# A hybrid HGRN2 / SSD block on one core: operands of the output projection turned as queued small products, and three smaller moves

## The chip, the cores and the metric

The kernel runs on one core of one Trainium2 chip, as one program. A core has a matrix engine (TensorE, PE in the profile, with PEld for its weight loads), VectorE (DVE), ScalarE (ACT), GpSimd (POOL) and SyncE (SP); each takes its own instructions strictly in their order and waits on semaphores for the others. Data move between HBM and the on-chip memory by DMA transfers, which SP, ACT or POOL issue. The metric is the time of one execution on the device, in microseconds (us); lower is better.

## The reference

One layer of a streaming encoder, for one sequence of 512 tokens of width 2048, all in float32:

```python
mod = silu(c) @ w_mod + b_mod                 # 2048 -> 6 x 2048
shift1, scale1, gate1, shift2, scale2, gate2 = split(mod, 6)
h = rms_norm(x, norm1_w) * (1 + scale1) + shift1
q, f, i, g, z, xbc, dt = split(h @ w_in)      # 4 x 1024, 1024, 2048, 16 columns
o_a = hgrn2_mixer(q, f, i, g)                 # 8 heads of 128, chunks of 64
o_b = ssd_mixer(z, xbc, dt)                   # 16 heads of 64 in 4 groups, state 128
x = x + gate1 * (concat(o_a, o_b) @ w_out)
h = rms_norm(x, norm2_w) * (1 + scale2) + shift2
u = causal_dwconv(h @ ffn_w_up)               # 2 x 5632, width 3
x = x + gate2 * ((silu(u_gate) * u_val) @ ffn_w_down)
return rms_norm(x, final_norm_w)
```

The SSD heads need, for each head and chunk, a matrix of decays `exp(acum[t] - acum[s])`, where `acum` is the running sum over time of `dt * a` of that head. The HGRN2 heads are a gated linear recurrence with its own decay for each of 128 channels; the kernel builds their attention matrix by doubling levels (1, 2, 4, ... 64).

## The kernel before

**Layout.** Tokens are 4 tiles of 128 (`NT`), the width 16 tiles of 128 (`KT`). For float32 accuracy every large product is three: an operand is split into a rounded part `hi` and a rest `lo`, and `mm3` issues hi x hi, hi x lo and lo x hi into the same PSUM bank (L168 to L170). Weights come through `wchunk`: SP loads two row tiles by 512 columns into a `raw` buffer (5 of them, L148), ACT rounds it to `whi` (L163), VectorE takes the difference `wlo` (L164); two `hi` and two `lo` buffers. `feat_group` and `tok_group` run a group of 512 columns over all 16 row tiles, eight chunks of 24 large products each, into 4 of 6 PSUM banks (`ACC`). Two more banks (`MIS`) serve all small products.

**Order of the work.** First the input is normed and transposed and the modulation of the first norm is summed; the SSD columns and the first half of the values `v` follow (`SEGMENTS`), then `v_group(1)`, four groups for the HGRN gates and queries (two heads each), two groups of `z`, two groups of `g`, the output projection (4 groups), the second norm, and the gated ConvFFN, which takes the second half of the time and which the change does not touch.

**The queue of small products.** The head mixers (`ssd_mix`, `hgrn_mix`) are Python generators that yield after small pieces. They stand in `waiting`; `small()`, called after every three large products, advances one of at most two active generators by one piece, so that small products stand between large ones in the program. A piece may ask to be left alone for some calls (`yield 3`). `drain()` advances until nothing is left.

**Modulation in the background.** `mod_unit` sums 512 columns of one of the six modulation vectors: eight loads `m` of 512 KB on SP (L184), which share the `raw` buffers, 16 multiply-adds on VectorE (L189, L191), then eight products with a column of ones that turn the sums (L203), and the addition into `modT` (L206). It yields after each load; the last multiply-adds and the column products follow in one step. `tick()`, called for each weight chunk, gives out `rate` steps: 0.5 in the gate and query groups, 1.5 from `z` to the output projection. `tick(99)` after the output projection does what is left. Twelve units run this way (scale2, gate1, shift2); four more (gate2) run in the FFN.

**The parts that the change touches.** `ssd_dt` turns the running sums so that they stand in 64 rows of 128 (chunk and head), and writes them to a DRAM tile `acrow` (L401). `decay(h)` in `ssd_mix` reads for one head four rows of 512 bytes, repeated for all 128 partitions, into a buffer `mm` (L436, issued by POOL), and makes the decay matrix from it (L439 to L443); L489 and L499 multiply with it and with the state, L494, L501 and L505 add the results into `y`. At the end of `hgrn_mix` three key tiles are transposed (L585), copied by ACT (L587) and multiplied into the states (L592), which VectorE evacuates (L595, L597); then ACT copies the reversed halves of the attention and query tiles into forward order (`fwd`, L602), and L612 and L615 form the output. `make_mix(kt)` transposes one of the 16 operand tiles of the output projection from `y` or `o` (four transposes, L859) and splits it (ACT L860, VectorE L861). In the kernel before it is a plain function, called in bursts of four behind the first `g` group, and of four and eight behind the second, where the queue is drained first. The residual `x` is loaded again behind that (`x1`, 4 x 1 MB on SP) and turned by `turn_x` through the queue (L897); `turn_x1` turns the result back (L905).

**What sets the final order.** A scheduler orders each engine's instructions before the run: it reckons with modelled durations and takes, of those that are ready, the one that stands first in the program (`tc.high_priority` moves some ahead). On the chip that order is fixed. Buffers come from pools by tag: 13 large ones `e`, 2 `y`, 2 `a`, and 9 of 512 columns (`T`); a new tile waits until an earlier one is released.

Of the kernel before, what the change touches and what calls it, by code (L numbers as in the profile page):

```python
# [7 lines left out]
F32 = mybir.dt.float32  # L8
F32R = mybir.dt.float32r
# [25 lines left out]
def hybrid_block_kernel(  # L35
# [140 lines left out]
    def mod_unit(part, j4):  # L176
# [4 lines left out]
        for q in range(9):  # L181
            if q < 8:
                m = wst.tile([P, 2, 512], F32, tag="raw", name=nm("m"))
                nc.sync.dma_start(out=m, in_=wmod[q * 256:(q + 1) * 256, c0:c0 + 512].rearrange(  # L184
                    "(k p) n -> p k n", p=P))
            for k in range(2 if q else 0):
                kt = 2 * q - 2 + k
                if kt == 0:
                    V.tensor_scalar(out=acc, in0=last[:, k, :], scalar1=cT[:, kt:kt + 1], scalar2=None, op0=ALU.mult)  # L189
                else:  # L190
                    V.scalar_tensor_tensor(out=acc, in0=last[:, k, :], scalar=cT[:, kt:kt + 1], in1=acc,  # L191
                                           op0=ALU.mult, op1=ALU.add)
            last = m
            if q < 8:
                yield
        ps = MIS()
# [160 lines left out]
    drm = ctx.enter_context(tc.tile_pool(name="drm", bufs=1, space=bass.MemoryType.DRAM))  # L357
    acrow = drm.tile([64, P], F32, tag="acrow", name="acrow")
    dtt = CT([P, 64], "dtt")
# [4 lines left out]
    def ssd_dt(src):  # L364
# [35 lines left out]
        V.tensor_copy(out=ar[0:64, 0:P], in_=pr[0:64, 0:P])  # L400
        nc.gpsimd.dma_start(out=acrow, in_=ar[0:64, 0:P])  # L401

    def ssd_mix(g):
# [29 lines left out]
        def decay(h):  # L433
            hh = 4 * g + h
            m = mt[h] = T("mm")
            nc.gpsimd.dma_start(out=m.rearrange("p (c t) -> p c t", c=4),  # L436
                                in_=acrow.rearrange("(c h) t -> h c t", h=16)[hh].partition_broadcast(P))
            m8 = m.rearrange("p (a t) -> p a t", a=8)
# [112 lines left out]
    def hgrn_mix(h, f, k, q):  # L551
# [12 lines left out]
        for lv in LEVELS:  # L564
# [15 lines left out]
            V.tensor_tensor(out=fb[:, :, :, 0, 0], in0=fb[:, :, :, 0, 0], in1=fb[:, :, :, 1, 0], op=ALU.mult)  # L580
            yield 3
        kt_ = T("Kt")[:, 0:3 * P]
        ps = MIS()
# [12 lines left out]
        for cch in (1, 2):  # L596
            V.scalar_tensor_tensor(out=st[:, cch * P:(cch + 1) * P], in0=st[:, (cch - 1) * P:cch * P],  # L597
                                   scalar=f[:, slot(cch).start:slot(cch).start + 1], in1=ps[:, cch * P:(cch + 1) * P],
                                   op0=ALU.mult, op1=ALU.add)
        fwd = T("fwd")  # L600
        for n, o in enumerate((att, q)):
            A.copy(out=fwd[:, n * 256:(n + 1) * 256].rearrange("p (c s) -> p c s", c=2),  # L602
                   in_=o[:, 256:512].rearrange("p (c s) -> p c s", c=2)[:, :, ::-1])

        def tokens(o, n, cch):
            return fwd[:, n * 256 + cch // 2 * P:n * 256 + (cch // 2 + 1) * P] if cch % 2 else o[:, slot(cch)]

        yield 1
# [52 lines left out]
    def feat_group(pieces, blocks, chunk_src=win, kts=range(0, KT, 2), accs=None, span=(0, KT),  # L661
                   rhs=None, kk_in=False):

        accs = accs or [ACC() for _ in blocks]
        rh, rl = rhs or (hhi, hlo)
        for k0 in kts:
            hi, lo = wchunk(chunk_src, k0, 2, pieces)
            tick()
# [181 lines left out]
    def make_mix(kt):  # L850
        q, j = divmod(kt, 4)
        if q not in mt_:
            mt_[q] = (E(F32R, "mhi"), E(F32R, "mlo"))
        hi, lo = mt_[q][0][:, j * 512:(j + 1) * 512], mt_[q][1][:, j * 512:(j + 1) * 512]
        mhi[kt], mlo[kt] = hi, lo
        src, col, w = (ov, kt, gnT[:, kt:kt + 1]) if kt < 8 else (yv, kt - 8, snT[:, kt - 8:kt - 7])
        ps = MIS()
        for t in range(NT):
            PE.transpose(out=ps[:, t * P:(t + 1) * P], in_=src(t)[:, col * P:(col + 1) * P], identity=ident)  # L859
        A.activation(out=hi, in_=ps, func=AF.Copy, scale=w)  # L860
        V.scalar_tensor_tensor(out=lo, in0=ps, scalar=w, in1=hi.bitcast(F32), op0=ALU.mult, op1=ALU.subtract)  # L861

    for j in range(2):
        accs = tok_group(win, C_G + 512 * j, hhi, hlo, list(range(KT)))
        if j:
            drain()
        for kt in range(8 + 4 * j, 12 + 4 * j):
            make_mix(kt)
        for t in range(NT):
# [7 lines left out]
    order = list(range(8, 16)) + list(range(0, 8))  # L877
    for kt in range(8):
        make_mix(kt)
    x1 = []  # L880
    for t in range(NT):
        x1t = E(name="x1")
        nc.sync.dma_start(out=x1t, in_=xd[t * P:(t + 1) * P, :])
        x1.append(x1t)
    x1T = []
    for q in range(4):
        x1T.append(E(name="x1T", tag=("y", "y", "a", "e")[q]))
    ssq2 = E(name="ssq2", tag="a")[:, 0:512]

# [3 lines left out]
    def turn_x(kt):  # L893

        ps = MIS()
        for t in range(NT):
            PE.transpose(out=ps[:, t * P:(t + 1) * P], in_=x1[t][:, kt * P:(kt + 1) * P], identity=ident)  # L897
            yield 0
        A.copy(out=x1f(kt), in_=ps)

    def turn_x1(q, t, bank):
# [8 lines left out]
    for n in range(4):  # L910
        accs = feat_group([(512 * n, 512)], [bl(i) for i in range(4)], chunk_src=wout, kts=order[::2], span=(8, 8),
                          rhs=(mhi, mlo), kk_in=True)
        with tc.high_priority(offset=2000 if n == 3 else 0):
# [168 lines left out]
```

## Time and profile before

| | us |
|---|---|
| median of 3 runs | 2491.99 (2491.88 to 2496.45) |
| the profiled execution | 2497.32 |
| its span, first to last instruction | 2495.6 |
| TensorE busy | 2416.4 (97%) |
| VectorE busy | 1490.2 (60%) |
| ScalarE busy | 783.7 (31%) |
| GpSimd busy | 55.7 (2%) |
| mean granted clock of TensorE | 0.991 |

In the rows of the profile `L436` is line 436 of the kernel, `mm<-acrow` means that the instruction writes tile `mm` and reads `acrow`, and `x16` that there were 16 of them. A large product shows as some 0.39 us busy but the next one starts 0.23 us after it, since products overlap; a busy TensorE is therefore not yet one at its peak. A row of the waits says which engine and tile waited, for whom, and how long in all, how often, and the longest. The granted clock is the share of TensorE's full clock in a stretch. A chain of waits follows the work that ended last back to what released it.

### The profile page before, as it was taken

What the parts mean: (1) busy time and instruction counts of PE and PEld (TensorE: products, weight loads), DVE (VectorE), ACT (ScalarE), POOL (GpSimd) and SP (SyncE); (2) the same over time, 40 slices, a digit from 0 to 9 for tenths busy, and PEclk for the clock granted to TensorE, in tenths of its full rate; (3) what the DMA queues carried; (4) which work ended last, traced back from release to release, by engine and by line L of the source; (5) the groups of instructions that cost most, each with busy time, mean ns of one, the idle gap of its engine ahead of it and who ended that gap; (6) DMA issues with size and microseconds to landing.
All of it is one profiled execution on the core that took longest, in us unless ns stands there. A gap on an engine that the chain in (4) does not pass through costs nothing.

```text
span 2495.6 us, 28998 instructions
## 1 busy us (share of the span) xinstructions
PE 2416.4 (97%) x11071; PEld 1987.7 (80%) x11071; DVE 1490.2 (60%) x2262; ACT 783.7 (31%) x1135; POOL 55.7 (2%) x80
## 2 busy tenths in 40 slices
PE   6999998999999999999999999999999999999998
PEld 5777877788777777887888888888888888888887
DVE  6884866666776656668536363636354545454557
ACT  6323422333332322433232222222222222222323
POOL 4000000000000000000000000000000000000000
PEclk9999999999999999999999999999999999999999
DMA  9883575344555656366333323233333333332332
GB/s 289 257 273 105 116 128 107 90 118 135 168 161 187 243 189 199 121 220 219 93 101 93 101 93 100 94 98 96 96 99 95 100 94 101 93 101 93 102 127 85
DMA packets 262823, 335.86 MB, mean 135 GB/s; under 512 B 18092, under 2 KB 182524, under 8 KB 261404
## 3 DMA queue, kind: packets, MB, share of 16 engines
q1 hardware_dynamic: 260432, 327.42, 41.8%
q0 software_dynamic: 1568, 4.31, 2.3%
q10 hardware_dynamic: 684, 2.28, 0.3%
q8 instruction: 87, 1.43, 0.2%
q14 instruction: 52, 0.43, 0.1%
HBM read 329.72 MB, written 4.23 MB: 134 GB/s over the span
## 4 chain that ended last, share of the span: by engine, by line
PE 76%; DMA 11%; DVE 9%; issue 2%; ACT 2%; POOL 0%; SPq 0%; DVEq 0%; ACTq 0%; POOLq 0%
PE acc L170 24%; PE acc L168 24%; PE acc L169 24%; DMA m<-in_w_mod_dram 8%; DVE wlo L164 3%; DVE macc L191 2%; DMA raw<-in_w_in_dram 1%; DVE macc L240 1%; DMA x<-in_x_dram 1%; ACT whi L163 1%; PE mis L570 1%; POOL rstd L267 0%; DMA mm<-acrow 0%; PE mis L612 0%; DVE att L577 0%
## 5 line engine op out<-in xcount | busy, mean ns | idle before, releaser
L164 DVE TENSOR_TENSOR wlo<-raw,whi 128x1024 fp32r<-128x1024 f32 (+1 forms) x408 | 490.3, 1203 | 707.7 <-ACT whi L163 703.2
L163 ACT CAST whi<-raw 128x1024 fp32r<-128x1024 f32 (+2 forms) x416 | 424.6, 1022 | 1304.4 <-PE acc L169 512.2
L168 PE MATMUL acc<-hhi,whi 128*128 128x512 f32 x1920 | 770.1, 402 | 10.7 <-ACT whi L163 6.1
L170 PE MATMUL acc<-hhi,wlo 128*128 128x512 f32 x1920 | 750.1, 393 | 3.1 <-DVE wlo L164 3.1
L169 PE MATMUL acc<-hlo,whi 128*128 128x512 f32 x1920 | 751.7, 392 | 0.0
L168 PEld LDWEIGHTS acc<-hhi,whi 128*128 128x128 f32 x1920 | 362.2, 189 | 88.2 <-ACT whi L163 10.2
L170 PEld LDWEIGHTS acc<-hhi,wlo 128*128 128x128 f32 x1920 | 362.3, 189 | 83.0 <-DVE wlo L164 6.1
L169 PEld LDWEIGHTS acc<-hlo,whi 128*128 128x128 f32 x1920 | 362.8, 189 | 69.5 <-issue 1.2
L191 DVE SCALAR_TENSOR_TENSOR macc<-m,cT,macc 128x512 f32<-128x512 f32 x240 | 180.0, 750 | 127.9 <-DMA m<-in_w_mod_dram 124.5
L168 PE MATMUL acc<-whi,act 128*128 128x512 f32 x640 | 249.0, 389 | 0.0
L169 PE MATMUL acc<-wlo,act 128*128 128x512 f32 x640 | 249.0, 389 | 0.0
L170 PE MATMUL acc<-whi,act 128*128 128x512 f32 x640 | 249.0, 389 | 0.0
L168 PE MATMUL acc<-whi,hhi 128*128 128x512 f32 x384 | 163.2, 425 | 0.0
L170 PE MATMUL acc<-whi,hlo 128*128 128x512 f32 x384 | 153.7, 401 | 0.0
L169 PE MATMUL acc<-wlo,hhi 128*128 128x512 f32 x384 | 152.8, 398 | 0.0
L170 PEld LDWEIGHTS acc<-whi,act 128*128 128x128 f32 x640 | 120.1, 188 | 25.0
L168 PEld LDWEIGHTS acc<-whi,act 128*128 128x128 f32 x640 | 120.1, 188 | 24.9
L169 PEld LDWEIGHTS acc<-wlo,act 128*128 128x128 f32 x640 | 120.1, 188 | 24.9
L994 DVE TENSOR_TENSOR g<-acc,gate 128x512 f32<-128x512 f32 x160 | 105.4, 685 | 3.8
L995 DVE TENSOR_TENSOR x<-x,g 128x512 f32<-128x512 f32 x160 | 105.3, 684 | 0.0
L168 PE MATMUL acc<-mhi,whi 128*128 128x512 f32 x256 | 105.2, 411 | 0.0
L170 PE MATMUL acc<-mhi,wlo 128*128 128x512 f32 x256 | 101.1, 395 | 2.3 <-DVE wlo L164 2.3
(274 smaller groups left out, 2193.9 us busy)
## 6 DMA issues: line engine op xcount, KB each, us to landing
raw<-in_ffn_w_up_dram SPq DMA_DIRECT2D x352, 256.0 KB, 2.9
m<-in_w_mod_dram SPq DMA_DIRECT2D x128, 512.0 KB, 4.1
raw<-in_ffn_w_down_dram SPq DMA_DIRECT2D x88, 512.0 KB, 3.6
m<-in_w_mod_dram SPq DMA_DIRECT2D x128, 256.0 KB, 4.2
raw<-in_w_in_dram SPq DMA_DIRECT2D x96, 256.0 KB, 3.9
raw<-in_w_in_dram SPq DMA_DIRECT2D x48, 512.0 KB, 4.0
raw<-in_w_out_dram SPq DMA_DIRECT2D x32, 512.0 KB, 4.5
x<-in_x_dram SPq DMA_DIRECT2D x8, 1024.0 KB, 10.8
```

The lines of the kernel that those rows point to most:

```text
L163: A.copy(out=h_, in_=r_)
L164: V.tensor_tensor(out=l_, in0=r_, in1=h_.bitcast(F32), op=ALU.subtract)
L168: PE.matmul(out=ps, lhsT=lh, rhs=rh, start=first, stop=False)
L169: PE.matmul(out=ps, lhsT=lh, rhs=rl, start=False, stop=False)
L170: PE.matmul(out=ps, lhsT=ll, rhs=rh, start=False, stop=last)
L191: V.scalar_tensor_tensor(out=acc, in0=last[:, k, :], scalar=cT[:, kt:kt + 1], in1=acc, op0=ALU.mult, op1=ALU.add)
L240: V.scalar_tensor_tensor(out=acc, in0=m[:, k, :], scalar=cT[:, kt:kt + 1], in1=acc, op0=ALU.mult, op1=ALU.add)
L570: PE.matmul(out=o, lhsT=kk[:, pr * P:(pr + 1) * P], rhs=halves(q, lv, True, base=pr * P, pairs=1), start=True, stop=True)
L994: V.tensor_tensor(out=m, in0=accs[t], in1=gates[5][:, cs], op=ALU.mult)
L995: V.tensor_tensor(out=x1[t][:, cs], in0=x1[t][:, cs], in1=m, op=ALU.add)
```

## The change

Four edits.

1. **Operands as queued small products.** `make_mix` becomes a generator that yields after each transpose. The eight SSD tiles are queued behind the first `g` group, after a `drain()` that stood behind the second; the eight HGRN tiles are queued behind the second. `need_mix(kt)` advances the queue until a pair of tiles is made; `feat_group` gets a hook `before` that calls it ahead of each chunk of the output projection. The turning of `x` is queued behind the operands, and a loop makes sure that the tiles of `x` that a group adds to have been turned. Some tiles change pools: the last pair of operand tiles is taken from `a`, `x1T` from `y` and `e`, and `ssq2` from `e`.
2. **Head operands ahead.** In `hgrn_mix` the two `fwd` copies stand ahead of the key transposes.
3. **Modulation sums a step later.** `mod_unit` also yields after the last multiply-adds, so that its column products come one step later.
4. **Decay rows by head.** `acrow` is 16 rows of 512 (one for each head); `decay` reads one row of 2 KB for each partition, and ACT issues the load.

```diff
@@ mod_unit
             last = m
-            if q < 8:
-                yield
+            yield
         ps = MIS()
@@
-    acrow = drm.tile([64, P], F32, tag="acrow", name="acrow")
+    acrow = drm.tile([16, S], F32, tag="acrow", name="acrow")
@@ ssd_dt
-        nc.gpsimd.dma_start(out=acrow, in_=ar[0:64, 0:P])
+        nc.gpsimd.dma_start(out=acrow.rearrange("h (c t) -> c h t", c=4), in_=ar[0:64, 0:P])
@@ ssd_mix, decay
-            nc.gpsimd.dma_start(out=m.rearrange("p (c t) -> p c t", c=4),
-                                in_=acrow.rearrange("(c h) t -> h c t", h=16)[hh].partition_broadcast(P))
+            nc.scalar.dma_start(out=m, in_=acrow[hh].partition_broadcast(P))
@@ hgrn_mix
+        fwd = T("fwd")
+        for n, o in enumerate((att, q)):
+            A.copy(out=fwd[:, n * 256:(n + 1) * 256].rearrange("p (c s) -> p c s", c=2),
+                   in_=o[:, 256:512].rearrange("p (c s) -> p c s", c=2)[:, :, ::-1])
...
         kt_ = T("Kt")[:, 0:3 * P]
...
-        fwd = T("fwd")
-        for n, o in enumerate((att, q)):
-            A.copy(out=fwd[:, n * 256:(n + 1) * 256].rearrange("p (c s) -> p c s", c=2),
-                   in_=o[:, 256:512].rearrange("p (c s) -> p c s", c=2)[:, :, ::-1])
...
@@ feat_group
-                   rhs=None, kk_in=False):
+                   rhs=None, kk_in=False, before=None):
...
         for k0 in kts:
+            if before:
+                before(k0)
             hi, lo = wchunk(chunk_src, k0, 2, pieces)
@@ make_mix
-            mt_[q] = (E(F32R, "mhi"), E(F32R, "mlo"))
+            mt_[q] = (E(F32R, "mhi", "a" if q == 3 else "e"), E(F32R, "mlo", "a" if q == 3 else "e"))
...
             PE.transpose(out=ps[:, t * P:(t + 1) * P], in_=src(t)[:, col * P:(col + 1) * P], identity=ident)
+            yield 0
...
+        made.add(kt)
+
+    made = set()
+
+    def need_mix(kt):
+        while not {kt, kt + 1} <= made:
+            small()
 
     for j in range(2):
         accs = tok_group(win, C_G + 512 * j, hhi, hlo, list(range(KT)))
-        if j:
+        if j == 0:
             drain()
-        for kt in range(8 + 4 * j, 12 + 4 * j):
-            make_mix(kt)
+            waiting.extend(make_mix(kt) for kt in range(8, 16))
...
-    for kt in range(8):
-        make_mix(kt)
-    x1 = []
+    waiting.extend(make_mix(kt) for kt in range(8))
+    for kt in range(8, KT, 2):
+        need_mix(kt)
+    x1, x1T, turned = [], [], set()
...
-    x1T = []
-    for q in range(4):
-        x1T.append(E(name="x1T", tag=("y", "y", "a", "e")[q]))
-    ssq2 = E(name="ssq2", tag="a")[:, 0:512]
+
+    sq2 = []
@@ turn_x
+        if kt % 4 == 0:
+            x1T.append(E(name="x1T", tag="y" if kt < 8 else "e"))
...
+        turned.add(kt)
@@ output projection
         accs = feat_group([(512 * n, 512)], [bl(i) for i in range(4)], chunk_src=wout, kts=order[::2], span=(8, 8),
-                          rhs=(mhi, mlo), kk_in=True)
+                          rhs=(mhi, mlo), kk_in=True, before=need_mix)
+        while not set(range(4 * n + 4)) <= turned:
+            small()
+        if not sq2:
+            sq2.append(E(name="ssq2")[:, 0:512])
+        ssq2 = sq2[0]
```

More of the change, by code (lines that the diff above doesn't have):

```diff
@@ L581, in hgrn_mix, with tokens @@
             yield 3
+        fwd = T("fwd")
+        for n, o in enumerate((att, q)):
+            A.copy(out=fwd[:, n * 256:(n + 1) * 256].rearrange("p (c s) -> p c s", c=2),
+                   in_=o[:, 256:512].rearrange("p (c s) -> p c s", c=2)[:, :, ::-1])
+        def tokens(o, n, cch):
+            return fwd[:, n * 256 + cch // 2 * P:n * 256 + (cch // 2 + 1) * P] if cch % 2 else o[:, slot(cch)]
         kt_ = T("Kt")[:, 0:3 * P]
@@ L599, in hgrn_mix @@
                                    op0=ALU.mult, op1=ALU.add)
-        fwd = T("fwd")
-        for n, o in enumerate((att, q)):
-            A.copy(out=fwd[:, n * 256:(n + 1) * 256].rearrange("p (c s) -> p c s", c=2),
-                   in_=o[:, 256:512].rearrange("p (c s) -> p c s", c=2)[:, :, ::-1])
-        def tokens(o, n, cch):
-            return fwd[:, n * 256 + cch // 2 * P:n * 256 + (cch // 2 + 1) * P] if cch % 2 else o[:, slot(cch)]
         yield 1
```

## Prediction

> **What bounds the kernel now.** I read the page's first and fourth parts, then stretches of the span, then TensorE's waits, then the chain inside the worst stretch. The profiled execution took 2497.3 us (its span and 1.7 us around it); the three timed runs have a median of 2491.99, 5.3 us less. My terms come from the trace and are subtracted from the median.
>
> ```profile
> span 2495.6 us, 28998 instructions
> ...
> PE 76%; DMA 11%; DVE 9%; issue 2%; ACT 2%; POOL 0%; SPq 0%; DVEq 0%; ACTq 0%; POOLq 0%
> ```
>
> TensorE carries three quarters of the chain, so only its idle time and its slow clock can be won; the change removes no product. Where that idle time lies, by stretches (columns: us, PE busy, PEld, DVE, ACT, POOL, granted clock, DMA share, GB/s):
>
> ```profile
> 300.00:350.00 50.00, 46.34 (x228) 38.01 (x227) 41.94 (x76) 15.31 (x21) 3.74 (x5) 0.99 0.73 111
> 350.00:400.00 50.00, 47.98 (x239) 38.77 (x239) 34.72 (x61) 13.74 (x19) 2.98 (x4) 0.98 0.55 125
> 400.00:450.00 50.00, 41.31 (x193) 33.72 (x193) 27.80 (x61) 12.71 (x16) 2.99 (x4) 0.94 0.59 105
> 500.00:550.00 50.00, 49.92 (x261) 41.63 (x260) 29.05 (x58) 19.56 (x53) 2.05 (x2) 1.00 0.39 111
> 750.00:800.00 50.00, 47.57 (x222) 39.37 (x221) 30.80 (x52) 14.52 (x24) 2.43 (x2) 1.00 0.59 188
> 800.00:850.00 50.00, 46.96 (x235) 38.47 (x234) 32.67 (x54) 17.46 (x23) 0.00 (x0) 1.00 0.66 224
> 1000.00:1050.00 50.00, 47.28 (x236) 39.82 (x235) 28.33 (x40) 20.73 (x32) 1.01 (x1) 0.97 0.39 122
> ```
>
> 300 to 450, where the SSD heads run between other products, loses 3.7 + 2.0 + 8.7 = 14.4 us of TensorE and, by the granted clock, 50 x (0.01 + 0.02 + 0.06) = 4.5 us more. The turning of the projection operands (750 to 850) loses 2.4 + 3.0. TensorE's own waits name the causes (total, times, longest, us):
>
> ```profile
> PE mis L499 <- DVE y L494: 7.9, 2, 4.2
> PE mis L499 <- DVE yo L501: 4.2, 1, 4.2
> PE mis L612 <- DVE st L597: 3.9, 2, 2.0
> PE mis L859 <- DVE mlo L861: 3.1, 2, 2.4
> PE mis L897 <- DMA x<-in_x_dram: 2.3, 1, 2.3
> PE mis L451 <- DVE cbm L429: 2.0, 2, 1.8
> PE mis L203 <- DVE st L597: 1.4, 1, 1.4
> ```
>
> L499 waits for VectorE to empty one of the two small PSUM banks. Why VectorE is late, the chain from 410 to 450 us says:
>
> ```profile
> 416.65 9.10 DMA m<-in_w_mod_dram
> 425.77 0.75 DVE macc L191
> ...
> 436.99 8.15 DMA mm<-acrow
> 445.16 0.69 DVE mm L439
> ...
> 446.77 0.70 PE mis L499 x2
> ```
>
> VectorE takes its work in order and stands before a modulation load (9.1 us) or a decay row (8.2 us), with the emptying of the bank behind it.
>
> **Decay rows by head.** Each of 16 loads today reads four 512-byte runs for every partition, issued from POOL; after the change it reads one 2 KB run, issued from ACT. The rows it goes by:
>
> ```profile
> q1 hardware_dynamic: 260432, 327.42, 41.8%
> q0 software_dynamic: 1568, 4.31, 2.3%
> q10 hardware_dynamic: 684, 2.28, 0.3%
> ...
> raw<-in_ffn_w_up_dram SPq DMA_DIRECT2D x352, 256.0 KB, 2.9
> m<-in_w_mod_dram SPq DMA_DIRECT2D x128, 512.0 KB, 4.1
> ...
> mm<-acrow POOLq DMA_DIRECT2D x16, 256.0 KB, 9.2
> ```
>
> The same 256 KB land in 2.9 us from SP and in 9.2 from POOL. Per MB, POOL's queue (q0) holds the DMA engines 2.3/4.31 = 0.53% of the span, SP's (q1) 0.13%, ACT's (q10) 0.13%. The 4.2 MB of decay rows thus cost about 2.2% of 2495.6 = 56 us of all engines, within the 160 us from 287 on; at q10's rate 14. So 42 us of engine time come free exactly where the modulation loads land late: a median of 4.1 us, but 9.1 in the chain above. I estimate 4 us to landing (between 2.9 and 9.2, nearer the first, since the queue kind and run length become those of the first). Five us come off each decay wait, and the modulation wait before 425.77 falls to its median. The three L499 waits and L451 sum to 14.1 us with a longest of 4.2: all are shorter than the five us. Bounds: 0 (VectorE's order still sets the waits) to 14.1. I take **10**, because the emptying of a bank still stands behind the decay arithmetic (L439, 0.69 us, and what follows). The slow clock follows the gaps: 0 to 4.5 us, I take **3**.
>
> What the issue costs on ACT, and POOL's issue for comparison:
>
> ```profile
> L259 ACTq DMA_DIRECT2D gate<-in_b_mod_dram x1: 396/396/396, 1039.3 to 1039.3; - x1
> ...
> L436 POOL DMA_DIRECT2D mm<-acrow x16: 747/747/804, 286.7 to 437.0; - x16
> ...
> ACT whi L163 <- PE acc L169: 512.2, 142, 7.4
> ...
> POOL mm L436 <- PE mis L489: 94.3, 5, 54.1
> ```
>
> 0.4 us x 16 = 6.3 us of ACT, which is busy at most 31% here. Behind an issue that waits for its buffer stand the weight casts (L163), for which TensorE waits. On POOL five issues waited for TensorE (L489), harmlessly. ACT's casts themselves wait for TensorE to free the weight buffers (512 us in all), so a hold until an earlier TensorE product costs 0; without that cover, five holds of up to one weight chunk (5.4 us) would cost 27. I take 0. The row write to DRAM (32 KB, now strided) has 24 us until the first read and costs nothing.
>
> **Projection operands as queued small products.** The 16 turnings keep their 64 transposes, 16 ACT copies (L860) and 16 VectorE ones (L861), but go between the big products, one per three. Today they come in bursts of eight and stop when both banks are full:
>
> ```profile
> 774.66 1.04 PE L859 MATMUL mis<-ident,y 128*128 128x128 f32 x8
> ...
> 777.36 0.39 PE L170 MATMUL acc<-whi,hlo 128*128 128x512 f32 x1
> 777.59 0.39 PE L168 MATMUL acc<-whi,hhi 128*128 128x512 f32 x1
> 780.40 0.66 PE L859 MATMUL mis<-ident,y 128*128 128x128 f32 x4 [2.43 <-DVE mlo L861]
> ...
> L615 PE MATMUL mis<-st,fwd x32: 270/274/358, 516.3 to 747.0; 128*128 128x128 f32 x32
> ```
>
> Gone: 3.1 us of L859. The x reload (four of 1 MB on SP) is first used about 40 small products later than today, some 30 us, so 2.3 us of L897 go too. The draining before the operands moves one group forward; the last head product today starts at 747.0 (L615), the first gate group, behind which the draining moves, ends where the first burst starts, at 774.7, so it finds the queue empty: 0. In exchange, two turnings at a time hold both banks, and each of the eight hand-overs needs VectorE on time, in a stretch where it waits for modulation loads. Bounds 0 to 8 x 2.43 = 19.4; nearest are the x turnings (L897), which hand over the same way and wait for their load alone, but ACT empties them. I take 3. Net **-2.4**. The moves between buffer pools keep 13 large buffers in use at most; 0.
>
> **Modulation sums a step later.** No TensorE wait is for a sum of theirs: the only L203 wait is for a bank (1.4 us), and that stays. Each of the 12 units needs 10 steps instead of 9, 120 against 108. Steps given out: 32 chunks at 0.5 and 64 at 1.5, 112. So 8 steps remain after the last chunk and come at once: six 512 KB loads, 14 multiply-adds, 8 column sums. Chunks are 24 products at 0.23 us, 5.4 us; the rows agree, since the last sums stand three chunks ahead of the last output-projection product:
>
> ```profile
> L203 PE MATMUL mis<-ones,macc x96: 164/250/271, 494.7 to 1011.0; 128*128 128x1 f32 x96
> ...
> L191 DVE SCALAR_TENSOR_TENSOR macc<-m,cT,macc x240: 741/752/758, 331.0 to 1169.8; 128x512 f32<-128x512 f32 x120
> ...
> 1027.33 0.40 PE L170 MATMUL acc<-mhi,wlo 128*128 128x512 f32 x1
> ```
>
> 14 x 0.752 = 10.5 us of VectorE around 1010 to 1040. Cover: 21.7 us of VectorE idle in 1000 to 1050, and a DMA share of 0.39. Without it they stand ahead of the second norm, whose statistics and operands are VectorE's: 0 to 10.5, I take **+1**.
>
> **Head operands copied ahead.** Two ACT copies per head (L602, 0.41 us each) go before the key copy. They are off the path: TensorE's waits at L612 are for the state evacuation on VectorE. Bounds: -3.9 (if those waits went) to +0.8 x 8 = 6.4 (if each key copy came that late unhidden; ACT is 39% busy in 500 to 550). I take 0.
>
> ```profile
> L602 ACT COPY fwd<-att x8: 402/406/408, 509.8 to 731.2; 128x256 f32<-128x256 f32 x8
> ```
>
> **Sum:** -10 - 3 - 2.4 + 1 = -14.4; 2491.99 - 14.4 = **2477.6**.
>
> **The rivals.**
>
> *The rows land no sooner.* The same 16 engines serve the same bytes, 55 to 73% busy there; only the issue gets cheaper, 0.35 us at each of four waits, 1.4 us. The time is then 2491.99 - 1.4 - 2.4 + 1 = 2489. For it: modulation loads on the fast queue also took 9 us. Against: q0's fourfold time per MB. The Trainium skill says so in "DMA: Bandwidth & Descriptors", section "Issuing engines are not separate DMA queues": starting a transfer from another engine saves only the issue. Here the run length changes as well, and the row of 9.2 against 2.9 us speaks against it. Chance 0.15.
>
> *All of it goes.* 14.1 + 4.5 + 5.4 us, with no hand-over wait and no tail: 2468. For it: all three causes are late DMAs. Chance 0.2.
>
> *The hand-overs cost more than the rows gain (slower).* Place: the second gate group and the first output group. Each hand-over waits for L861 behind a multiply-add that waits for a load. At 2.43 us plus a full 4.1 us load each, 8 x 6.5 = 52 us, less the 5.4 and 13 that go: +34. With half of them late, 26 - 18.4 = +8, 2500, which I take. It is slower from 18.4/8 = 2.3 us per hand-over on. Against: the scheduled order places a transpose where its bank is reckoned free. Chance 0.1.
>
> **How the numbers follow.** My forecast has 0.55 (2470 to 2487), the others 0.15, 0.2 and 0.1. A measurement here tells 0.2%, 5 us, from no change: same is 2487 to 2497. Faster: 0.55 x 0.95 + 0.2 + a little of the first rival, 0.74. Same: the rest of that rival and of the forecast, 0.15. Slower: 0.11, the last rival and some order that the scheduler upsets. The range 2464 to 2496 takes all four terms at their best, 24 us plus 3.9 of L612, and most of the first rival; it leaves out the slower one.
>
> **What would show it.** Decay rows landing in 3 to 5 us on ACT's queue, L499 waits below 4 us in all, and the granted clock at 0.98 or more in 400 to 450. L859 waits below 3 us and none at L897 for x. A last L203 start within a few us of the last output-projection product, and 1000 to 1050 no worse than 47.3 us of TensorE. I am wrong if L499 waits as before, or if TensorE's waits at L859 and L203 pass 15 us.

## The result

The changed kernel takes 2481.53 us in the median (2478.29 to 2483.98, 5 runs), the kernel before 2496.45 us beside it (2491.88 to 2498.66, 5 runs): a ratio of 0.9947, 95% interval [0.9935, 0.9958]. The prediction was 2477.6 us, 0.9942 of the median it was made against. The profiled execution took 2480.27 us, 1.7 us more than its span.

From the page of the changed kernel, the span, ACT's queue (packets, MB, share of 16 engines) and the chain by engine:

```profile
span 2478.6 us, 28956 instructions
...
q10 hardware_dynamic: 2988, 6.47, 0.8%
...
PE 80%; DMA 8%; DVE 8%; ACT 2%; issue 1%; SPq 0%; POOL 0%; ACTq 0%; DVEq 0%; POOLq 0%
```

From its view of transfers, the decay rows (KB each, median us to landing):

```profile
mm<-acrow ACTq DMA_DIRECT2D x16, 256.0 KB, 4.5
```

They land in half the time, TensorE's share of the chain rises from 76 to 80%, and transfers fall from 11 to 8%. TensorE's own waits for small products, once 7.9 and 4.2 us at L499 (now L497), 3.1 at L859 and 2.3 at L897 (now L905), are these, as far as they bear on the change:

```profile
PE mis L449 <- DVE y L456: 2.9, 2, 1.5
PE mis L914 <- ACT x L916: 2.8, 2, 2.2
...
PE mis L610 <- DVE st L603: 1.5, 2, 1.1
PE acc L914 <- ACT x L916: 1.4, 1, 1.4
PE mis L202 <- DVE mlo L862: 1.3, 1, 1.3
...
PE mis L202 <- ACT o L618: 1.3, 1, 1.3
PE acc L914 <- DVE x1T L930: 0.7, 1, 0.7
...
PE mis L497 <- DVE y L492: 0.5, 1, 0.5
...
PE mis L497 <- DVE yo L499: 0.5, 1, 0.5
```

Where the time went, by stretches: the SSD heads (280 to 460) and the output projection (860 to 1020). The columns are those of the prediction's table. Before:

```profile
280.00:460.00 180.00, 165.63 (x800) 135.32 (x799) 129.28 (x234) 58.49 (x83) 12.02 (x16) 0.97 0.62 116
860.00:1020.00 160.00, 156.28 (x729) 126.72 (x729) 89.95 (x117) 41.87 (x52) 0.00 (x0) 1.00 0.59 191
```

After, with the two stretches that the prediction had named:

```profile
280.00:460.00 180.00, 176.09 (x879) 144.96 (x878) 136.73 (x247) 63.71 (x91) 0.00 (x0) 1.00 0.40 120
860.00:1020.00 160.00, 152.71 (x721) 122.72 (x719) 95.73 (x125) 46.04 (x61) 0.00 (x0) 0.98 0.61 194
...
400.00:450.00 50.00, 49.54 (x249) 40.96 (x248) 31.30 (x68) 18.66 (x29) 0.00 (x0) 1.00 0.39 117
...
1000.00:1050.00 50.00, 45.37 (x235) 37.50 (x235) 43.43 (x64) 25.92 (x39) 1.01 (x1) 1.00 0.49 154
```

In 280 to 460 TensorE's idle time falls from 14.4 to 3.9 us, its clock rises from 0.97 to 1.00, and the DMA engines' share falls from 0.62 to 0.40 at the same bytes per second. Fixed places in the work show how much of that arrives. The groups by line of the kernel before give the first product of the HGRN heads, which follow the SSD heads, and the last one of the output projection (min/median/max ns, first and last start):

```profile
L557 PE MATMUL mis<-q,FK x64: 270/273/324, 460.1 to 681.7; 128*128 128x128 f32 x64
...
L170 PE MATMUL acc<-mhi,wlo x256: 387/389/504, 825.9 to 1027.3; 128*128 128x512 f32 x128
```

The same two places and the last modulation sums in the changed kernel:

```profile
L555 PE MATMUL mis<-q,FK x64: 270/273/321, 445.1 to 668.8; 128*128 128x128 f32 x64
...
L170 PE MATMUL acc<-mhi,wlo x256: 388/393/628, 807.8 to 1011.3; 128*128 128x512 f32 x128
...
L202 PE MATMUL mis<-ones,macc x96: 164/250/352, 494.5 to 1012.2; 128*128 128x1 f32 x96
```

The changed kernel leads by 460.1 - 445.1 = 15.0 us when the SSD heads are done, by 1027.3 - 1011.3 = 16.0 at the end of the output projection, and by 2495.6 - 2478.6 = 17.0 at the end. Nearly all of the gain is made before 445 us. In between, the passage to the second norm gives back 1.6 us: with the large products (L168 to L170) counted in their order, the 3600th, behind that passage, starts 14.4 us earlier than before. The last 17.0 - 14.4 = 2.6 us come in the FFN's first group (below).

### The profile page after: what moved, and what is told of

Its sections match the earlier page's. It is cut to its first block, busy times and chain, and to the rows that moved or that the text cites. A ratio compares the mean times of both kernels' runs of the same rounds, so it can differ in the third digit from the quotient of the medians.

```text
span 2478.6 us, 28956 instructions
## 1 busy us (share of the span) xinstructions
PE 2414.0 (97%) x11071; PEld 1982.7 (80%) x11071; DVE 1494.3 (60%) x2262; ACT 786.4 (32%) x1135; POOL 43.4 (2%) x64
## 3 DMA queue, kind: packets, MB, share of 16 engines
q10 hardware_dynamic: 2988, 6.47, 0.8%
## 4 chain that ended last, share of the span: by engine, by line
PE 80%; DMA 8%; DVE 8%; ACT 2%; issue 1%; SPq 0%; POOL 0%; ACTq 0%; DVEq 0%; POOLq 0%
PE acc L168 25%; PE acc L170 25%; PE acc L169 25%; DMA m<-in_w_mod_dram 6%; DVE wlo L164 2%; DVE macc L191 2%; DVE macc L239 1%; DMA raw<-in_w_in_dram 1%; PE mis L568 1%; ACT whi L163 1%; DMA raw<-in_ffn_w_up_dram 1%; DMA mm<-acrow 0%; DMA x<-in_x_dram 0%; PE mis L487 0%; PE mis L202 0%
## 5 line engine op out<-in xcount | busy, mean ns | idle before, releaser
L168 PE MATMUL acc<-hhi,whi 128*128 128x512 f32 x1920 | 767.8, 401 | 8.7 <-ACT whi L163 4.6
L170 PE MATMUL acc<-hhi,wlo 128*128 128x512 f32 x1920 | 747.7, 391 | 4.3 <-DVE wlo L164 4.2
L168 PEld LDWEIGHTS acc<-hhi,whi 128*128 128x128 f32 x1920 | 361.3, 188 | 86.3 <-ACT whi L163 8.7
L170 PEld LDWEIGHTS acc<-hhi,wlo 128*128 128x128 f32 x1920 | 360.6, 188 | 83.9 <-DVE wlo L164 8.0
L168 PE MATMUL acc<-whi,act 128*128 128x512 f32 x640 | 249.0, 389 | 0.0
L170 PE MATMUL acc<-whi,act 128*128 128x512 f32 x640 | 249.0, 389 | 0.0
L168 PE MATMUL acc<-whi,hhi 128*128 128x512 f32 x384 | 165.2, 431 | 0.0
L170 PE MATMUL acc<-whi,hlo 128*128 128x512 f32 x384 | 152.7, 398 | 0.0
L170 PEld LDWEIGHTS acc<-whi,act 128*128 128x128 f32 x640 | 120.2, 188 | 25.1 <-issue 0.2
L168 PEld LDWEIGHTS acc<-whi,act 128*128 128x128 f32 x640 | 120.2, 188 | 25.0
L168 PE MATMUL acc<-mhi,whi 128*128 128x512 f32 x256 | 111.5, 435 | 0.0
L170 PE MATMUL acc<-mhi,wlo 128*128 128x512 f32 x256 | 101.9, 398 | 1.6 <-DVE wlo L164 1.6
```

The costliest lines, as they stand in the source:

```text
L168: PE.matmul(out=ps, lhsT=lh, rhs=rh, start=first, stop=False)
L170: PE.matmul(out=ps, lhsT=ll, rhs=rh, start=False, stop=last)
```

## The experiments

Each kernel ran beside the kernel before on one chip; ratios are to that. "Stage" is TensorE's busy time in 280 to 460 us, "landing" the median of the 16 decay rows.

| kernel | median us | ratio, 95% interval | stage us | landing us |
|---|---|---|---|---|
| changed kernel | 2481.53 | 0.9947 [0.9935, 0.9958] | 176.1 | 4.5 |
| decay edit alone | 2482.81 | 0.9936 [0.9917, 0.9955] | 175.8 | 4.7 |
| 2 KB runs, issued from POOL | 2475.94 | 0.9906 [0.9882, 0.9929] | 179.7 | 3.8 |
| 512-byte runs, issued from ACT | 2520.02 | 1.0089 [1.0068, 1.0110] | 153.3 | 9.5 |
| all edits but the decay's | 2496.09 | 0.9996 [0.9985, 1.0008] | 164.7 | 9.5 |
| sums in the old step | 2482.37 | 0.9938 [0.9925, 0.9951] | | |
| copies behind the transposes | 2478.20 | 0.9923 [0.9910, 0.9936] | | |
| turnings in bursts | 2485.21 | 0.9938 [0.9924, 0.9952] | | |
| changed + idle loads, same rows | 2482.83 | 0.9941 [0.9922, 0.9961] | 171.1 | 6.2 |
| changed + idle loads, own rows | 2479.12 | 0.9922 [0.9900, 0.9944] | 175.0 | 4.5 |
| changed, rows from POOL | 2476.23 | 0.9906 [0.9893, 0.9918] | 179.0 | 4.0 |
| the same, queue at 0.75 | 2474.33 | 0.9910 [0.9893, 0.9928] | 178.4 | 4.0 |

### Which of the edits pays

The decay edit alone, put into the kernel before:

```diff
-    acrow = drm.tile([64, P], F32, tag="acrow", name="acrow")
+    acrow = drm.tile([16, S], F32, tag="acrow", name="acrow")
...
-            nc.gpsimd.dma_start(out=m.rearrange("p (c t) -> p c t", c=4),
-                                in_=acrow.rearrange("(c h) t -> h c t", h=16)[hh].partition_broadcast(P))
+            nc.scalar.dma_start(out=m, in_=acrow[hh].partition_broadcast(P))
```

> The kernel before with the decay rows by head as its only edit (16 rows of 512 in DRAM, one 2 KB run for each partition, issued from ACT). Theory: the decay rows carry the change, so it is 13 to 15 us faster than the kernel before (ratio 0.994 to 0.995), rows land in 3 to 6 us instead of 9.2, and TensorE's idle time from 280 to 460 us falls from 14.4 us to about 4. Rival: the four edits share the gain, then this one alone gives 5 to 8 us (0.997 to 0.998).

And the other three edits without it, its lines taken back in the changed kernel:

```diff
-    acrow = drm.tile([16, S], F32, tag="acrow", name="acrow")
+    acrow = drm.tile([64, P], F32, tag="acrow", name="acrow")
...
-            nc.scalar.dma_start(out=m, in_=acrow[hh].partition_broadcast(P))
+            nc.gpsimd.dma_start(out=m.rearrange("p (c t) -> p c t", c=4),
+                                in_=acrow.rearrange("(c h) t -> h c t", h=16)[hh].partition_broadcast(P))
```

> The changed kernel without the decay edit: decay rows as in the kernel before, the other three edits (turned operands, copies ahead, sums a step later) in place. Theory (the whole gain is the decay's, the other three come to zero within 3 us): ratio 0.998 to 1.001 of the kernel before, TensorE busy in 280 to 460 about 165.6 us. Rival (the three edits gain by themselves, as the prediction's -2.4 us for the operand turnings says): ratio 0.9965 to 0.9985, 4 to 8 us below the kernel before.

The decay edit alone gives 0.9936, the rest without it 0.9996, whose interval holds 1. In the stage, the first row is of the decay edit alone:

```profile
280.00:460.00 180.00, 175.83 (x880) 144.88 (x880) 136.58 (x251) 62.85 (x90) 0.00 (x0) 1.00 0.42 123
```

and this one of the other three edits:

```profile
280.00:460.00 180.00, 164.69 (x789) 134.75 (x788) 127.08 (x230) 56.28 (x75) 12.01 (x16) 0.95 0.62 114
```

So the whole measured gain is the decay rows'. The other three come to -1.0 us (0.9996 x 2499), between -3.7 and +2.0.

### Run length or queue

The edit changes two things at once: the runs (four of 512 bytes for each partition, now one of 2 KB) and the engine that issues (POOL, now ACT). Each was tried alone in the kernel before. Longer runs, still from POOL:

```diff
-    acrow = drm.tile([64, P], F32, tag="acrow", name="acrow")
+    acrow = drm.tile([16, S], F32, tag="acrow", name="acrow")
...
+            nc.gpsimd.dma_start(out=m, in_=acrow[hh].partition_broadcast(P))
```

> The kernel before with the rows by head (2 KB runs), but still issued from POOL. If the run of 512 bytes was what made the rows land late, they land in 4 to 5 us and the whole 13 to 15 us are gained. If it was POOL's queue, they still land in 8 to 9 us, that queue keeps some 2% of the DMA engines' span, and the gain is 0 to 3 us.

The old runs, issued from ACT:

```diff
-            nc.gpsimd.dma_start(out=m.rearrange("p (c t) -> p c t", c=4),
+            nc.scalar.dma_start(out=m.rearrange("p (c t) -> p c t", c=4),
                                 in_=acrow.rearrange("(c h) t -> h c t", h=16)[hh].partition_broadcast(P))
```

> The kernel before with its four runs of 512 bytes, but issued from ACT. If POOL's queue made the rows late, they land in 4 to 5 us and 13 to 15 us are gained. If the runs of 512 bytes did, they land in 8 to 9 us and the gain is 0 to 3 us.

The transfers, first with 2 KB runs from POOL:

```profile
q0 software_dynamic: 1584, 4.31, 0.6%
...
mm<-acrow POOLq DMA_DIRECT2D x16, 256.0 KB, 3.8
```

then with 512-byte runs from ACT:

```profile
q10 hardware_dynamic: 9132, 6.47, 1.1%
...
mm<-acrow ACTq DMA_DIRECT2D x16, 256.0 KB, 9.5
```

Of the two, the run length decides when the rows land, and the queue does not. With 2 KB runs POOL's queue lands in 3.8 us and holds the engines 0.6 / 4.31 = 0.14% of the span per MB, as SP's does; the 0.53% of the prediction belonged to the runs. With 512-byte runs ACT's queue lands in 9.5 us, and the kernel is slower than before by 0.9%, where the forecast was a gain of 0 to 3 us. TensorE's waits in the stage then are

```profile
PE mis L451 <- DVE y L458: 14.9, 2, 9.5
PE mis L499 <- DVE y L494: 11.6, 2, 7.4
```

The issuing engine is thus not without effect on the time. The kernel before has the same runs and nearly the same landing (9.2 us) from POOL; issuing them from ACT costs 0.0089 x 2498 = 22 us. VectorE waits 19.4 us for the rows in the stage there, and 4.7 us from POOL.

The Trainium skill's rule that the issuing engine saves only issue time ("DMA: Bandwidth & Descriptors", "Issuing engines are not separate DMA queues") agrees with the landings of both runs; of the 22 us it says nothing. It did not speak against the change, because the runs changed too.

POOL even beats ACT. In the changed kernel with the issue put back:

```diff
-            nc.scalar.dma_start(out=m, in_=acrow[hh].partition_broadcast(P))
+            nc.gpsimd.dma_start(out=m, in_=acrow[hh].partition_broadcast(P))
```

> The changed kernel with its 2 KB rows issued from POOL again. From the two kernels that differ in the same way without the other edits (2475.9 from POOL, 2482.8 from ACT): 4 to 7 us faster than the changed kernel, rows landing in 3.8 us. Rival: that difference was the scatter of runs; then within 2 us.

Its ratio is 0.9906, and its interval lies wholly below the changed kernel's, which was measured in another session; the medians differ by 5.3 us, the ratios by 10, and the two kernels with the decay edit alone, on one chip, by 6.9. The waits in 280 to 460 us show a part of it. Kernel before:

```profile
DVE macc L191 <- DMA m<-in_w_mod_dram: 18.1, 4, 6.2
...
DVE mm L439 <- DMA mm<-acrow: 4.7, 1, 4.7
```

Changed kernel:

```profile
ACT whi L163 <- DMA mm<-acrow: 9.4, 2, 6.6
...
DVE macc L191 <- DMA m<-in_w_mod_dram: 7.5, 4, 3.9
DVE mm L437 <- DMA mm<-acrow: 6.9, 7, 1.7
...
ACT mm L440 <- DMA mm<-acrow: 4.6, 1, 4.6
```

With the rows from POOL:

```profile
DVE macc L191 <- DMA m<-in_w_mod_dram: 7.9, 4, 3.7
DVE mm L437 <- DMA mm<-acrow: 1.0, 1, 1.0
```

From POOL no wait of ACT ends with a decay row, and VectorE waits 1.0 us for them instead of 6.9. On ACT the rows are asked for in ACT's order, behind its casts and copies: the first goes out at 307.4 us, from POOL at 286.3. TensorE is busy 179.0 us of the stage instead of 176.1, and the first product of the HGRN heads starts at 441.2 us instead of 445.1, so 3 to 4 us of the gain lie there. The two profiled executions as a whole are only 1.6 us apart; where the rest of the gain lies, these traces can't say.

Against the kernel before, the changed kernel has shorter waits for the modulation loads (7.5 us for 18.1), not for the rows themselves (6.9 for 4.7), although the rows land in half the time. From POOL both are short.

### Why short runs are dear

The first question was whether the short runs cost time by holding the DMA engines, or only because the rows themselves came late. The changed kernel got 16 loads that nothing reads, three 512-byte runs for each partition, the same three rows for all:

```diff
+            nc.gpsimd.dma_start(out=idle.rearrange("p (c t) -> p c t", c=3),
+                                in_=arow2.rearrange("(c h) t -> h c t", h=16)[hh, 0:3].partition_broadcast(P))
```

> The changed kernel, with, beside each decay load, a load from POOL of three runs of 512 bytes for each partition into a buffer that nothing reads (three quarters of the old traffic, 16 x 192 KB). Nothing waits for these loads. Theory that the old loads hurt by holding the DMA engines: modulation loads land late again between 290 and 440 us, TensorE's idle time from 280 to 460 us rises from 3.9 us by 4 to 8, the time by 5 to 10 us. Rival that only the wait for the rows themselves cost time: within 2 us of the changed kernel.

In the stage the theory held: TensorE's idle time rises from 3.9 to 8.9 us, and the HGRN heads start at 449.3 us instead of 445.1. In the time it did not: 2482.83 us cannot be told from the changed kernel's. Of this lag of 4.2 us, 2.5 are left at the end of the profiled execution (spans of 2481.1 and 2478.6 us).

The next question was what makes such loads dear, the number of runs or that all partitions read the same rows. A first try at other addresses read the rows of `x`:

```diff
+            nc.gpsimd.dma_start(out=idle.rearrange("p (c t) -> p c t", c=3),
+                                in_=xd[0:P, :].rearrange("p (c t) -> p c t", t=P)[:, 0:5:2, :])
```

> The changed kernel with the 16 idle loads of 512-byte runs (nothing reads what they bring; their rows in the tile are not used), but from different addresses of x instead of the same three rows of the decay for every partition. Theory (the number of runs sets the price): as with the same rows, TensorE's busy time in 280 to 460 is about 171 us (idle 8 to 10 us), the waits of the sums on modulation loads there about 15 us, the idle loads land in 6 to 8 us. Rival (many partitions that read one row of memory collide there): TensorE 175 to 177 us busy as in the changed kernel, the waits on modulation loads 6 to 9 us, the idle loads land in under 5 us.

It answered nothing about the stage: `x` is ready at once, so all 16 loads went out between 1.4 and 90.9 us, and the SSD heads began 21 us late (309.0 for 288.1); 2505.63 us in its only run. Its transfers say something all the same: as many short runs from POOL, each partition from its own row of `x`, landed in 4.4 us, and 3.30 MB held the engines 0.4% of the span, 0.12% per MB. The second try writes a table of its own rows when the decay sums are ready, and every partition reads its own:

```diff
+        for b in (0, 64):
+            for k in (0, 2, 4):
+                nc.gpsimd.dma_start(out=adist[b:b + 64, k * P:(k + 1) * P], in_=ar[0:64, 0:P])
...
+            nc.gpsimd.dma_start(out=idle.rearrange("p (c t) -> p c t", c=3),
+                                in_=adist.rearrange("p (c t) -> p c t", t=P)[:, 0:5:2, :])
```

> The changed kernel with 16 idle loads of three 512-byte runs per partition (192 KB each, nothing reads them), as in the run with idle loads, but every partition reads its own row of a table written from the decay sums, instead of all partitions the same three rows. Where a load comes from memory so decides, the number of runs being the same (384). Theory (the number of runs sets the price): the idle loads land in 6 to 8 us, as 7.3 us from the same rows; TensorE is busy about 171 us of 280 to 460 against 176 in the changed kernel, and the sums' waits on modulation loads there are 12 to 18 us. Rival (runs of many partitions from one row of memory collide there, and the number of runs is not what counts): the idle loads land in 3 to 5 us, TensorE is busy 175 to 177 us, and the waits on modulation loads are 6 to 9 us.

The transfers with the same rows for all partitions:

```profile
q0 software_dynamic: 1360, 3.30, 2.3%
...
mm<-acrow ACTq DMA_DIRECT2D x16, 256.0 KB, 6.2
...
idle<-arow POOLq DMA_DIRECT2D x16, 192.0 KB, 7.3
```

with own rows:

```profile
q0 software_dynamic: 1520, 3.46, 0.5%
...
mm<-acrow ACTq DMA_DIRECT2D x16, 256.0 KB, 4.5
...
idle<-adist POOLq DMA_DIRECT2D x16, 192.0 KB, 3.3
```

and their stage, the same rows first:

```profile
280.00:460.00 180.00, 171.08 (x846) 140.41 (x844) 130.52 (x238) 60.08 (x86) 9.69 (x13) 0.98 0.64 135
```

then own rows:

```profile
280.00:460.00 180.00, 175.01 (x866) 143.83 (x865) 134.13 (x244) 61.75 (x88) 8.22 (x11) 0.99 0.45 133
```

The theory that the number of runs sets the price fell: the rival's numbers came. With as many runs of the same length from the same queue, own rows land in 3.3 us and hold the engines 0.5 / 3.46 = 0.14% of the span per MB; the same rows take 7.3 us and 2.3 / 3.30 = 0.70%. On POOL's queue, then, it is not the number of the short runs that is dear but where they lie. Two things differ there: all partitions read the same rows or each its own, and a partition's runs stand 8 KB apart or 1 KB. The cheap loads from `x` had 8 KB between the rows of neighbouring partitions, which speaks against the spacing, but it was not varied by itself; that the shared rows are the cause is likely and not shown. The Trainium skill's line rate from 512 bytes on ("DMA: Bandwidth & Descriptors", "Specifications") agrees with the own rows and differs from the shared ones by five times; the measurement decides. The loads of shared rows also hurt others: beside them the decay rows land in 6.2 us instead of 4.5, and the sums' waits on modulation loads in the stage, 7.5 us in the changed kernel, are

```profile
DVE macc L191 <- DMA m<-in_w_mod_dram: 15.4, 4, 8.3
```

with the shared rows, and 7.8 with own ones.

Two things stay open. What collides in memory, and why 128 reads of one 2 KB row go free, no run shows. And on ACT's queue the short runs land as late (9.5 us) although they hold the engines far less there: with them that queue's share rises from 0.3% (2.28 MB, in the kernel before) to 1.1% (6.47 MB), 0.19% per MB. That share counts the time of packets, and a load is 528 packets there, one for each of its 512 runs and 16 more, against 80 from POOL; what passes between packets is not in it. So what delays the runs on ACT is open, and own rows were not tried on it.

### The other three edits, each undone in the changed kernel

The sums in the old step:

```diff
-            yield
+            if q < 8:
+                yield
```

> The changed kernel with the modulation sums in their old step (9 steps for each unit). Theory: the later sums cost the tail behind the output projection, 1 to 2 us, so this is 0 to 2 us faster than the changed kernel, and the last column products stand at least 10 us ahead of the last output-projection product. Rival: the later sums spare TensorE waits; then it is 2 us or more slower.

The copies behind the key transposes:

```diff
-        fwd = T("fwd")
...
         kt_ = T("Kt")[:, 0:3 * P]
...
+        fwd = T("fwd")
...
         yield 1
```

> The changed kernel with the two copies of the head operands behind the state products, as before. Theory: they are off the path, within 1.5 us of the changed kernel. Rival: the waits at the head outputs come back (3.9 us in the kernel before, 1.5 in the changed one), 2 to 4 us slower.

The turnings as a plain function in bursts, with the old buffers:

```diff
-        if j == 0:
+        if j:
             drain()
-            waiting.extend(make_mix(kt) for kt in range(8, 16))
+        for kt in range(8 + 4 * j, 12 + 4 * j):
+            make_mix(kt)
...
-    waiting.extend(make_mix(kt) for kt in range(8))
-    for kt in range(8, KT, 2):
-        need_mix(kt)
+    for kt in range(8):
+        make_mix(kt)
```

> The changed kernel with the operand turnings in bursts as before (the other three edits stay). Theory: the queue wins its waits back (L859 and x, 5.4 us) and loses as much at the turning back of x, so within 2 us of the changed kernel, with L859 waits of 3 to 4 us again and none of 2 us at the turning back. Rival: the queue gained 4 to 5 us by itself, then this is 4 to 5 us slower.

The first and the third cannot be told from the changed kernel. With the copies behind, the ratio is lower by 0.0024 and the intervals only just touch, so that the copies ahead may cost something, and the forecast of no more than 1.5 us either way is not borne out; all three overlap with the decay edit alone. What the edits do to the waits is in the traces. Bursts bring the old waits back:

```profile
PE acc L169 <- DVE hlo L291: 3.1, 1, 3.1
...
PE mis L857 <- DVE mlo L859: 2.3, 1, 2.3
PE mis L895 <- DMA x<-in_x_dram: 1.9, 1, 1.9
```

Sums in the old step end at 994.8 us, 16 us ahead of the last output product, and spare the passage to the second norm: from the 3400th to the 3600th large product it takes 59.0 us, 60.9 in the changed kernel and 58.3 in the kernel before. But then TensorE waits for the operand splits 4.7 + 2.1 us at the sums and at the turnings. Copies behind the transposes add 0.9 us of waits at L610.

### A version that beats both

With the rows from POOL, the queue was also let through at 0.75 steps a chunk instead of 0.5 in the gate and query groups, so that nothing is left behind the output projection:

```diff
-        rate[0] = 0.5
+        rate[0] = 0.75
```

> The changed kernel with two edits: the decay rows in 2 KB runs issued from POOL (2476 us, ratio 0.9906, by themselves), and the small products of the queue let through at 0.75 a step instead of 0.5 in the groups that carry them, so that nothing of the queue is left for after the last output projection. Theory (the end of the sums is now all that stands between the projections and the next stage, 1.4 us behind the last output projection product, and the transition lost 1.7 us): 2473 to 2476 us, ratio 0.989 to 0.991, at most 2 us better than without the rate. Rival (a denser queue makes TensorE wait for VectorE's sums and for the turned operands in the same groups): L859, L914 and L202 waits grow by 3 us or more together, and the time is 2478 us or above, ratio over 0.991.

2474.33 us, 0.991 [0.9893, 0.9928]: faster than the changed kernel and the kernel before, and no different from rows from POOL alone. In the trace the last sums stand at 1001.9 us, 5 us ahead of the last output-projection product, and the same passage to the second norm takes 59.0 us, against 62.8 with the slower rate. In return TensorE waits 6.4 us at L202 for VectorE, 3.6 more than with the slower rate, while its waits at L914 fall from 5.1 to 0.3 us. L859, L914 and L202 together come to 7.2 us for 7.9, so neither the rival's waits nor its time came.

## Why the prediction was right, and where it was wrong

**The decay rows were the change.** -10 for the waits and -3 for the clock were predicted; the lead at the end of the SSD heads is 15.0 us, and the ratio of the edit alone gives 0.0064 x 2498 = 16 us (11 to 21). The waits were sized well: TensorE's idle time fell by 10.5 us, and the L499 waits of 12.1 us became 1.0. The way there was only in part the one described. "Five us come off each decay wait", it says; the landing fell by 4.7 us, but VectorE's waits for the rows did not fall (4.7 us in the stage before, 6.9 after). What fell are its waits for the modulation loads, 18.1 to 7.5 us, the second half of the prediction's sentence. The term mis-sized is the clock. It was put at 3 of at most 4.5, but the granted clock in 400 to 450 rose from 0.94 to 1.00 and over 280 to 460 from 0.97 to 1.00, which is up to 180 x 0.03 = 5.4 us, and 15.0 - 10.5 leaves 4.5 for it. It goes with the gaps: in this stage it is 0.91 where TensorE is idle 26.7 us (short runs from ACT), 0.95 at 15.3, 0.98 at 8.9 and 1.00 at 3.9.

**The step that failed is the reason given for it.** The landing of 4 us was to come "since the queue kind and run length become those of the first", and the 42 us of engine time from "q0's fourfold time per MB". The size came (4.5 us, a DMA share of 0.40 for 0.62), but the queue kind has no part in it: POOL with 2 KB runs lands in 3.8 us, ACT with 512-byte runs in 9.5 and makes the kernel slower. The prediction took two rows that differed in queue, run length and place in memory (SP's weights at 2.9 us, POOL's decay rows at 9.2) and gave the difference to all of them at once. That the run length goes with the price is shown. What makes short runs dear was looked at on POOL's queue alone: there it is where the runs lie, most likely that many partitions read the same short rows.

**ACT's issue, taken as 0, costs 5 to 10 us** against POOL's with the same rows. The cover named was that ACT's casts wait for TensorE anyway, so that an issue which waits behind them costs nothing. The casts are indeed covered: TensorE waits for none of them in the stage. What was not counted is the other side, the rows themselves: asked for in ACT's order, they are late for VectorE (6.9 us against 1.0), and the emptying of a bank stands behind them (TensorE's 2.9 us at L449, which are gone from POOL). The bound of 27 held. The row that should have set the choice was POOL's five waits of 94 us, harmless on an engine with nothing else to do.

**The turnings: -2.4 predicted, about 0 measured.** What was to go went: no L859 wait, no wait for `x`, and 1.4 us at the old L905 for a modulation sum besides, 6.8 us in all. What came was not the hand-over waits at L859 that were costed at +3, but 6.2 us one step further on, where the result is turned back and the sums turned (L914 and L202 in the waits above). The chain of waits of the changed kernel says why:

```profile
907.15 4.90 DMA m<-in_w_mod_dram
912.15 0.76 DVE macc L191
...
913.72 3.59 DMA m<-in_w_mod_dram
...
918.07 0.69 DVE ssq L937
918.76 0.67 DVE x1T L930
...
920.61 0.47 PE mis L914
```

VectorE stands before two modulation loads, 8.5 us, and the turned result waits behind it: the same pattern as at L499, moved to the next place where a bank needs VectorE. In this stretch the clock fell to 0.98, which is 3 us more of 160. Counted in large products, the lead over the kernel before grows from 17.6 us at the 2600th to 23.3 at the 2900th, by the waits that went, and is 14.1 at the 3100th. With the turnings in bursts it is 16.1 and 15.8 at the last two, with the sums in their old step 16.9 and 14.2, so in these traces the large fall comes only where both edits meet.

**Sums a step later: +1 predicted, 1.6 measured** in the passage to the second norm. The mechanism is in the main as described: the last sums stand 0.9 us behind the last output-projection product, but the multiply-adds left over come ahead of it, from 996 to 1011 us, and not from 1010 to 1040. VectorE's work around it rises from 28.3 us (1000 to 1050) to 37.2 (984 to 1034 in the changed kernel, the same work 16 us earlier). The test set for it, TensorE no worse than 47.3 us busy there, failed with 45.4 in either stretch. **Copies ahead: 0**, and nothing that the runs resolve.

**Not foreseen: 2.6 us gained in the FFN, by the same edit.** There the same work leaves the kernel before waiting once and running slower behind it:

```profile
1143.15 0.50 PE L168 MATMUL acc<-hhi,whi 128*128 128x512 f32 x1 [2.36 <-ACT whi L163]
```

No TensorE wait stands there in the changed kernel; it loses 1.7 us shortly before this place and wins 4.5 at it. The text ahead of the prediction says that the change does not touch the FFN, and the prediction counts 12 modulation units; but `mod_unit` also makes the four units of gate2 that run in the FFN, and their sums come a step later too. The runs tell the edits apart: a wait of 2.3 to 3.0 us stands at this place in all five kernels with the sums in their old step (3.0 us in the changed kernel with that edit alone undone), and in none of the nine with the sums a step later. How the later step spares this wait is not shown.

**The sum came out in part by luck.** The medians measured side by side differ by 14.9 us, the prediction said 14.4. But the decay rows gave 2 us more than forecast, the 2.4 us of the turnings did not come, and the 2.6 us in the FFN were in no term.

**The rivals.** "The rows land no sooner" fell with the landing. "All of it goes" came true in the stage (3.9 us of idle time left) but not behind it. "The hand-overs cost more" fell: no wait at L859, and the three edits together at 0.9996.

## What to carry to other kernels

A load that lands late should be asked for its access pattern before its queue: from POOL, many partitions that read the same few short rows cost five times the engine time of as many own rows, and one longer run for each partition removes it. Compare the same work and not the same time on the clock when a change moves all that follows: here 1000 to 1050 us was other work before and after. A transfer belongs on an engine whose order holds nothing that others wait for; a cheaper issue on a busy engine was worth less than a dearer one on an idle one. When a stall before an engine that works in order is moved, look for the next piece of work that stands behind the same loads.

## What the hardware showed that was not expected

- Runs of 512 bytes from three rows read by all 128 partitions landed in 7.3 us per 192 KB and held the engines five times as long per MB as runs of 512 bytes from own rows, which landed in 3.3 us. Number, length and queue of the runs were the same; the distance between a partition's runs was not (8 KB and 1 KB).
- The same 512-byte pattern on ACT's queue landed as late, 9.5 us, with less packet time on the engines (0.19% of the span per MB against 0.53% on POOL's), in 528 packets a load instead of 80.
- Idle loads that nothing waits for doubled the waits of another engine's loads, from 7.5 to 15.4 us, when their rows were shared, and left them at 7.8 when they were not.
